# Attention without GpSimd: weights' lower halves on VectorE, probabilities scaled by ScalarE and VectorE

## The chip, the cores and the metric

The kernel runs on one core of a Trainium2 chip. The metric is the device time of one execution in microseconds. The kernel before has a median of 2958.11 us over three runs (2956.08 to 6801.14 us).

## The reference, cut to what matters

One inference step of a decoder trunk of four layers, for a prompt of 512 positions and a sample group of 8 rows: sparse attention (NSA), gMLP, HGRN2, sparse attention again, each followed by a SwiGLU FFN and layer norms. The change touches the two attention layers, and of these the prompt group. There are 16 query heads in 4 key-value groups of 4, of width 64. Each branch (compressed, selected, window) makes a masked softmax and adds its product with the values, times a gate:

```
s = einsum('bqgrd,bkgd->bqgrk', q, k) * ATTN_SCALE
p = where(mask, softmax(where(mask, s, NEG_INF)), 0)
o_branch = einsum('bqgrk,bkgd->bqgrd', p, v)
o = gates[0] * o_cmp + gates[1] * o_slc + gates[2] * o_win
```

With 512 positions every block of 64 is selected, so the selected and the window branch are plain causal attention over their own keys and values. The factor gate / sum of the softmax is applied to the probabilities.

## The kernel before, in words

Activations lie transposed: 128 features on the partitions, 520 columns (512 prompt positions and 8 sample rows) in two halves of 256 and 264. A matrix product in full precision is made of three TensorE passes over halves of the operands: upper by upper (L344), lower by upper (L345), upper by lower (L346). The upper half is a copy rounded to TensorE's format, the lower half what the rounding left out.

**Weights.** `Weights.need` (called by `mm` before each group of products) keeps a few parts of 512 columns split ahead of use (three in the attention layers, `ahead`). A part comes by DMA on SyncE's queue, `split` has ScalarE copy the upper half (L148) and at once, as `lag` is off there, another engine subtract (L150). That engine is VectorE, unless `self.sub` names another. In `nsa`, once tile 9 of the 21 tiles of the input projection is reached (L1507), `sub` names GpSimd for both parts of a tile, and it is set back after the output projection (L1532): the parts of u_in from tile 9 on, two for each tile, and the 16 of u_out.

**The order of work.** Each engine carries out its instructions in the order in which the program wrote them. The input projection (`mm`, 21 tiles, two halves) calls `tick` after every second k-step; a tick advances generators: `compress` (summaries of the cached pages, L1050 among them), from tile 9 on `attend`, four steps for each tick. So projection products, attention and splits lie between each other by the order of writing, not by readiness. When the projection is done, `attend` goes on beside `sample` (the 8 sample rows) and, with its later half, beside the output projection.

**Attention.** `attend` goes over 4 groups g, 4 query blocks qb of 128 and 3 branches. For the selected and the window branch `scores` handles four heads i: two score products (L1176) of n = 128, 256, 384 or 512 key columns, on VectorE the mask and the row minimum in one instruction (L1178; signs are turned), one step later on ScalarE the exp with its sum (L1180). Then VectorE makes reciprocal and factor (L1184, L1185), and each head's probabilities are multiplied by their factor: head 0 on GpSimd, head 1 on ScalarE (L1189), heads 2 and 3 on VectorE (L1192). This happens 32 times in a layer, eight times for each n. Two rounds later `mix` transposes the probabilities on TensorE (L1211), ScalarE takes the upper half out (L1214), VectorE the lower half (L1215), and TensorE multiplies by the values (L1227).

**Around it on VectorE:** the evacuation of keys (L1452 to L1457; L1453 and L1454 each subtract 64 x 256, L1454 reading the one operand from the upper and the other from the lower partitions), of queries (L1472, L1476), the compressed branch (L1149 to L1162), the split of the attention's result (L306) and residual sums (L488, L469). L1283 scales the probabilities of the sample rows.

Of the kernel before, what the change touches and what calls it, by code (L numbers as in the profile page):

```python
# [11 lines left out]
OP = mybir.AluOpType  # L12
# [51 lines left out]
def wait(n):  # L64
    for _ in range(n):
        yield
# [169 lines left out]
class Net:  # L236
# [773 lines left out]
    def nsa(self, layer, plan):  # L1010
        nc, a = self.nc, self.a
# [99 lines left out]
        def attend():  # L1111
# [3 lines left out]
            def defer(f):  # L1115
                due.append([DEFER, f])
# [49 lines left out]
            def scores(g, qb, br):  # L1166
                q0, n = qb * 128, qb * 128 + 128
                nn = max(n, 256)
                kt = K[g, br]
                Ps = [self.slot(), self.slot()]  # L1170
                st = self.small("nst", 8, bufs=4)
                for i in range(4):
                    p = self.ps()
                    q = Q[g, i // 2][:, i % 2, q0:n]
                    for s in range(2):
                        nc.tensor.matmul(p[:, :nn], q, kt[:, s, :nn], start=s == 0, stop=s == 1)  # L1176
                    P = Ps[i // 2][:, i % 2, :n]
                    nc.vector.tensor_tensor_reduce(P, p[:, :n], tri[:, 512 - n:], 1.0, 3e38, OP.add, OP.min,  # L1178
                                                   st[:, i:i + 1])
                    defer(lambda P=P, i=i: (self.table(LN_EXP), nc.scalar.activation(  # L1180
                        P, P, AF.Exp, bias=st[:, i:i + 1], scale=-1.0, accum_out=st[:, 4 + i:5 + i])))
                    yield
                yield from wait(DEFER)
                nc.vector.reciprocal(st[:, 4:8], st[:, 4:8])  # L1184
                nc.vector.tensor_mul(st[:, 4:8], st[:, 4:8], gt[:, qb, 16 * br + 4 * g:16 * br + 4 * g + 4])  # L1185
                for i in range(4):
                    P = Ps[i // 2][:, i % 2, :n]
                    if i == 1:
                        nc.scalar.activation(P, P, AF.Copy, scale=st[:, 4 + i:5 + i])  # L1189
                    else:  # L1190
                        eng = nc.gpsimd if i == 0 else nc.vector
                        eng.tensor_scalar(P, P, st[:, 4 + i:5 + i], None, op0=OP.mult)  # L1192
                D[g, qb, br] = Ps
                yield

# [47 lines left out]
            for g, qb, br in [(g, qb, br) for g in range(4) for qb in range(4) for br in range(3)]:  # L1243
                if qb == br == 0:
                    while g not in done or "prompt" not in done:
                        yield
                    oT[g] = self.slot()
                    late.append(values(g))
                late.append(mix(g, qb, br))
                cur = [scores(g, qb, br) if br else scores_cmp(g, qb)]  # L1250
                while len(late) > LAG:
                    cur.append(late.pop(0))
                for _ in alternate(cur[0], chain(*cur[1:])):
                    flush()
                    yield
# [230 lines left out]
        for i, (m, h) in enumerate(self.order(21, 6, 0)):  # L1486
            if i == 4:
                cst = self.small("ncst", 672)
                nc.scalar.dma_start(cst, a["nsa_cst"])
                tri = cst[:, :512]  # L1490
                cmask = cst[:, 512:640].rearrange("p (q c) -> p q c", q=4)
                valid = cst[:, 640:641]
                m8, gm = cst[:, 641:649], cst[:, 649:653]
                brsel, hsel = cst[:48, 653:656], cst[:48, 656:672]
                kcS = self.sm.tile([128, 2, 2, 9, 32], FT, name="kcS", tag="kcS", bufs=1)
                nc.gpsimd.memset(kcS, 0.0)
                zero = self.flat()
                nc.gpsimd.memset(zero, 0.0)
                KV, PTC2 = self.flat(FR), [self.slot(FR), self.slot(FR)]
                nc.vector.tensor_copy(KV, zero)  # L1500
                for t in PTC2:
                    nc.vector.tensor_copy(t.rearrange("p a b -> p (a b)"), zero)
                VC = KV[:, 512:1024].rearrange("p (g c) -> p g c", g=4)
                Qd = self.sm.tile([128, 2, 8, 16], FT, name="Qd", tag="Qd", bufs=1)
                nc.gpsimd.memset(Qd, 0.0)
            if m == 9 and h == 0:
                self.W.sub = (nc.gpsimd, nc.gpsimd)  # L1507
                att = self.spawn(attend(), RATE)
            p = self.mm(u_in[m], 8, X, h)
            evac(m, h, p)  # L1510
# [141 lines left out]
```

## Time and profile before

| | before |
|---|---|
| median of the runs | 2958.11 us |
| profiled execution | 2956.41 us |
| its span, first to last instruction | 2954.7 us |
| mean granted TensorE clock | 0.978 of full speed |
| instructions on TensorE, VectorE, ScalarE, GpSimd | 21806, 4377, 3586, 674 |

The profile is that of one execution. PE is TensorE's matmuls and PEld its weight loads, DVE VectorE, ACT ScalarE, POOL GpSimd, SP SyncE. L150 is line 150 of the kernel. Time points count from the span's start. Busy TensorE is not TensorE at its peak, since matmuls overlap. The first attention layer lies at about 15 to 440 us, the second at about 2120 to 2540 us. Two instructions on one engine can overlap by a little, so a pair can be shorter than twice one.

### The profile page before, as it was taken

What the parts mean: (1) busy time and instruction counts of PE and PEld (TensorE: products, weight loads), DVE (VectorE), ACT (ScalarE), POOL (GpSimd) and SP (SyncE); (2) the same over time, 40 slices, a digit from 0 to 9 for tenths busy, and PEclk for the clock granted to TensorE, in tenths of its full rate; (3) what the DMA queues carried; (4) which work ended last, traced back from release to release, by engine and by line L of the source; (5) the groups of instructions that cost most, each with busy time, mean ns of one, the idle gap of its engine ahead of it and who ended that gap; (6) DMA issues with size and microseconds to landing.
All of it is one profiled execution on the core that took longest, in us unless ns stands there. A gap on an engine that the chain in (4) does not pass through costs nothing.

```text
span 2954.7 us, 56446 instructions
## 1 busy us (share of the span) xinstructions
PE 2766.9 (94%) x21806; PEld 2642.0 (89%) x21806; DVE 2011.7 (68%) x4377; ACT 1591.5 (54%) x3586; POOL 731.9 (25%) x674
## 2 busy tenths in 40 slices
PE   7999888999999999999999989999899998899997
PEld 7888568999999899999999989999888875899997
DVE  5788757665766775677676677557768876575665
ACT  4666545554565464465455556446566655463553
POOL 0222141342321223232000022323112212322342
PEclk9999999999999999999999999999999999999998
DMA  5122533555523255562222235556122243445561
GB/s 180 65 65 70 181 121 94 144 154 147 154 79 102 61 138 138 139 185 80 81 88 81 71 93 143 140 139 190 60 83 65 65 160 123 118 114 137 148 158 53
DMA packets 167678, 340.38 MB, mean 115 GB/s; under 512 B 15474, under 2 KB 78450, under 8 KB 167410
## 3 DMA queue, kind: packets, MB, share of 16 engines
q1 hardware_dynamic: 147840, 281.79, 30.1%
q0 software_dynamic: 12096, 44.05, 8.6%
q10 hardware_dynamic: 7474, 10.95, 1.0%
q8 instruction: 171, 2.80, 0.4%
q14 instruction: 97, 0.79, 0.1%
HBM read 323.46 MB, written 13.27 MB: 114 GB/s over the span
## 4 chain that ended last, share of the span: by engine, by line
PE 71%; DVE 15%; ACT 9%; issue 2%; DMA 2%; SPq 1%; POOL 0%; ACTq 0%; POOLq 0%; DVEq 0%
PE ps L344 11%; PE ps L346 11%; PE ps L345 11%; PE ps L566 9%; PE ps L567 9%; PE ps L568 8%; PE ps L1050 2%; PE ps L1227 2%; PE ps L1176 1%; ACT g L1180 1%; DVE g L1178 1%; ACT g L380 1%; PE ps L873 1%; PE ps L1211 1%; DVE g L150 1%
## 5 line engine op out<-in xcount | busy, mean ns | idle before, releaser
L344 PE MATMUL ps<-g 128*128 128x256 f32 (+1 forms) x3744 | 1093.7, 292 | 26.8 <-ACT g L148 21.0
L346 PE MATMUL ps<-g 128*128 128x256 f32 (+1 forms) x3744 | 1071.3, 286 | 16.2 <-DVE g L411 14.3
L345 PE MATMUL ps<-g 128*128 128x256 f32 (+1 forms) x3744 | 1067.6, 285 | 5.6 <-DVE g L150 2.9
L344 PEld LDWEIGHTS ps<-g 128*128 128x128 f32 x3744 | 718.1, 192 | 41.8 <-ACT g L148 22.3
L346 PEld LDWEIGHTS ps<-g 128*128 128x128 f32 x3744 | 715.6, 191 | 19.7 <-DVE g L411 17.0
L345 PEld LDWEIGHTS ps<-g 128*128 128x128 f32 x3744 | 717.2, 192 | 12.7 <-DVE g L150 4.4
L150 DVE TENSOR_TENSOR g<-g 128x512 fp32r<-128x512 f32 x708 | 578.7, 835 | 152.1 <-ACT g L148 149.1
L566 PE MATMUL ps<-g 128*128 128x260 f32 x2128 | 601.8, 283 | 7.5 <-ACT frow L613 7.5
L567 PE MATMUL ps<-g 128*128 128x260 f32 x2128 | 601.6, 283 | 0.0
L568 PE MATMUL ps<-g 128*128 128x260 f32 x2128 | 601.1, 282 | 0.0
L148 ACT CAST g<-g 128x512 fp32r<-128x512 f32 (+1 forms) x788 | 460.6, 607 | 121.8 <-PE ps L346 86.9
L566 PEld LDWEIGHTS ps<-g 128*128 128x128 f32 x2128 | 401.2, 189 | 8.3 <-ACT frow L613 8.3
L568 PEld LDWEIGHTS ps<-g 128*128 128x128 f32 x2128 | 401.6, 189 | 0.0
L567 PEld LDWEIGHTS ps<-g 128*128 128x128 f32 x2128 | 401.1, 189 | 0.0
L613 ACT ACTIVATE frow<-ps 128x260 f32<-128x260 f32 x304 | 118.1, 388 | 245.8 <-PE ps L568 245.6
L1180 ACT ACTIVATE g<-g,nst 128x128 f32<-128x128 f32 (+3 forms) x256 | 143.1, 559 | 127.7 <-DVE nst L1178 125.5
L150 DVE TENSOR_TENSOR g<-fsum,g 128x512 fp32r<-128x512 f32 x228 | 163.4, 717 | 35.2 <-ACT g L148 35.2
L622 POOL TENSOR_TENSOR frow<-frow 128x260 f32<-128x260 f32 x64 | 47.9, 749 | 520.4 <-ACT frow L613 520.4
L150 POOL TENSOR_TENSOR g<-g 128x512 fp32r<-128x512 f32 x80 | 105.7, 1328 | 255.7 <-ACT g L148 249.4
L1192 POOL TENSOR_SCALAR g<-g,nst 128x128 f32<-128x128 f32 (+3 forms) x64 | 76.3, 1192 | 351.0 <-DVE nst L1185 243.4
L148 ACT CAST g<-fsum 128x512 fp32r<-128x512 f32 x228 | 133.9, 616 | 48.8 <-PE ps L346 48.8
L488 DVE SCALAR_TENSOR_TENSOR x<-x,ps 128x256 f32<-128x256 f32 (+1 forms) x128 | 53.2, 422 | 152.7 <-PE ps L346 152.7
(270 smaller groups left out, 4061.6 us busy)
## 6 DMA issues: line engine op xcount, KB each, us to landing
g<-ffn_in SPq DMA_DIRECT2D x176, 512.0 KB, 4.7
g<-ffn_in POOLq DMA_DIRECT2D x76, 512.0 KB, 5.9
g<-ffn_out SPq DMA_DIRECT2D x64, 448.0 KB, 3.8
g<-nsa_in SPq DMA_DIRECT2D x42, 512.0 KB, 4.0
fsum<-ffn_in SPq DMA_DIRECT2D x76, 256.0 KB, 3.5
cm<-cache_cmp SPq DMA_DIRECT2D x64, 256.0 KB, 3.7
g<-cache_slc SPq DMA_DIRECT2D x128, 128.0 KB, 2.5
g<-cache_win SPq DMA_DIRECT2D x32, 512.0 KB, 5.7
```

The lines of the kernel that those rows point to most:

```text
L148: self.nc.scalar.copy(h, src)
L150: self.subs.append(lambda: (eng or self.nc.vector).tensor_sub(l, src, h.bitcast(FT)))
L344: nc.tensor.matmul(p[:, :n], H[:, s], a, start=k == 0, stop=False)
L345: nc.tensor.matmul(p[:, :n], L[:, s], a, start=False, stop=False)
L346: nc.tensor.matmul(p[:, :n], H[:, s], b, start=False, stop=k == nk - 1)
L566: nc.tensor.matmul(p, H[:, s], a, start=start and k == 0, stop=False, skip_group_check=True)
L567: nc.tensor.matmul(p, L[:, s], a, start=False, stop=False, skip_group_check=True)
L568: nc.tensor.matmul(p, H[:, s], b, start=False, stop=k == 3, skip_group_check=True)
L613: nc.scalar.activation(s[q], p, AF.Copy, scale=-1.0 if q in (1, 5) else 1.0)
L1050: nc.tensor.matmul(p[:, :8 * n], WC[kv][:, l], cv[:, :n, kv, l, :], start=l == 0, stop=l == 7)
L1180: defer(lambda P=P, i=i: (self.table(LN_EXP), nc.scalar.activation(P, P, AF.Exp, bias=st[:, i:i + 1], scale=-1.0, accum_out=st[:, 4 + i:5 ...
L1192: eng.tensor_scalar(P, P, st[:, 4 + i:5 + i], None, op0=OP.mult)
```

## The change

Two places. In `scores`, head 0 is scaled by ScalarE, as head 1 is, and no longer by GpSimd; heads 2 and 3 stay on VectorE. In `nsa`, `sub` is no longer set, so that all lower halves of weights are subtracted by VectorE. Order of writing, tiles and DMAs stay as they are.

```diff
@@ -1185,11 +1185,10 @@
                 for i in range(4):
                     P = Ps[i // 2][:, i % 2, :n]
-                    if i == 1:
+                    if i < 2:
                         nc.scalar.activation(P, P, AF.Copy, scale=st[:, 4 + i:5 + i])
                     else:
-                        eng = nc.gpsimd if i == 0 else nc.vector
-                        eng.tensor_scalar(P, P, st[:, 4 + i:5 + i], None, op0=OP.mult)
+                        nc.vector.tensor_scalar(P, P, st[:, 4 + i:5 + i], None, op0=OP.mult)
@@ -1504,7 +1503,6 @@
             if m == 9 and h == 0:
-                self.W.sub = (nc.gpsimd, nc.gpsimd)
                 att = self.spawn(attend(), RATE)
```

## Rows read from the trace of the kernel before

**Rows 1.** the page: totals; groups (count, busy us, mean ns, idle before)
```profile
PE 2766.9 (94%) x21806; PEld 2642.0 (89%) x21806; DVE 2011.7 (68%) x4377; ACT 1591.5 (54%) x3586; POOL 731.9 (25%) x674
...
L150 POOL TENSOR_TENSOR g<-g 128x512 fp32r<-128x512 f32 x80 | 105.7, 1328 | 255.7 <-ACT g L148 249.4
L1192 POOL TENSOR_SCALAR g<-g,nst 128x128 f32<-128x128 f32 (+3 forms) x64 | 76.3, 1192 | 351.0 <-DVE nst L1185 243.4
```

**Rows 2.** windows: stretch, length, busy us (instructions) by engine, clock, DMA
```profile
85.00:300.00 215.00, 194.19 (x1383) 176.48 (x1383) 179.57 (x545) 142.02 (x373) 55.90 (x46) 0.98 0.22 66
300.00:400.00 100.00, 85.94 (x564) 59.88 (x563) 69.11 (x218) 55.76 (x144) 22.47 (x20) 0.93 0.49 151
```

**Rows 3.** the chain of waits, 85 to 300 us, by line
```profile
by line: ACT g L1180 8.6%; DVE g L1178 8.4%; PE ps L345 4.8%; PE ps L346 4.8%; issue 4.8%; PE ps L344 4.8%; PE ps L1227 4.7%; PE ps L1176 4.5%; DVE g L1454 4.5%; DVE g L1215 4.2%; PE ps L1050 4.2%; PE ps L1211 4.1%; DVE g L1192 3.9%; DVE g 
```

**Rows 4.** waits, 85 to 300 us: who <- for whom: us, times, longest
```profile
DVE nst L1184 <- ACT g L1180: 17.9, 24, 1.1
...
DVE g L1178 <- PE ps L1176: 1.9, 2, 1.0
...
ACT g L1180 <- DVE nst L1178: 42.3, 45, 3.7
...
PE ps L1211 <- POOL g L1192: 4.0, 2, 2.5
```

**Rows 5.** timeline, 202 to 205 us: start, us, engine, line, operation
```profile
202.67 0.62 ACT L148 CAST g<-g 128x512 fp32r<-128x512 f32 x1
...
202.62 0.28 DVE L1149 TENSOR_TENSOR g<-ps,ncst 128x128 f32<-128x128 f32 x1
...
203.47 1.28 DVE L1215 TENSOR_TENSOR g<-ps,g 128x512 fp32r<-128x512 f32 x2
```

**Rows 6.** timeline, 169 to 172 us, VectorE and GpSimd
```profile
169.79 1.40 DVE L1454 TENSOR_TENSOR g<-g 64x256 fp32r<-64x256 f32 x1
...
169.48 1.43 POOL L150 TENSOR_TENSOR g<-g 128x512 fp32r<-128x512 f32 x1 [2.68 <-PE ps L1176]
```

**Rows 7.** line groups with shapes kept apart, 60 to 440 us
```profile
L1454 DVE TENSOR_TENSOR g<-g 64x256 fp32r<-64x256 f32 x13 | 11.4, 877 | 0.2
...
L1453 DVE TENSOR_TENSOR g<-g 64x256 fp32r<-64x256 f32 x13 | 5.4, 418 | 0.4
...
L1283 DVE TENSOR_SCALAR g<-g,sst 128x513 f32<-128x513 f32 x2 | 1.0, 488 | 0.1
```

**Rows 8.** line groups with shapes together, 60 to 440 us
```profile
L1180 ACT ACTIVATE g<-g,nst 128x128 f32<-128x128 f32 (+3 forms) x128 | 71.5, 559 | 64.6 <-DVE nst L1178 63.6 <-DVE g L1380 0.7
...
L1192 DVE TENSOR_SCALAR g<-g,nst 128x128 f32<-128x128 f32 (+3 forms) x64 | 32.0, 542 | 1.1
...
L1189 ACT ACTIVATE g<-g,nst 128x128 f32<-128x128 f32 (+3 forms) x32 | 18.0, 563 | 14.8 <-DVE nst L1185 14.8
```

**Rows 9.** timeline: pairs of L1192 on VectorE, and GpSimd beside them
```profile
134.09 1.32 DVE L1192 TENSOR_SCALAR g<-g,nst 128x512 f32<-128x512 f32 x2
...
134.22 1.79 POOL L1192 TENSOR_SCALAR g<-g,nst 128x512 f32<-128x512 f32 x1 [1.11 <-DVE nst L1185]
...
162.83 0.48 DVE L1192 TENSOR_SCALAR g<-g,nst 128x128 f32<-128x128 f32 x2
...
166.04 0.60 DVE L1192 TENSOR_SCALAR g<-g,nst 128x128 f32<-128x128 f32 x2
...
254.84 1.63 DVE L1192 TENSOR_SCALAR g<-g,nst 128x256 f32<-128x256 f32 x2
...
254.99 1.33 POOL L150 TENSOR_TENSOR g<-g 128x512 fp32r<-128x512 f32 x1 [6.22 <-ACT g L148]
```

**Rows 10.** the chain of waits, 140 to 153 us, by line
```profile
by line: PE ps L1050 27.5%; PE ps L1227 14.4%; PE ps L346 13.9%; PE ps L1211 13.4%; PE ps L344 13.0%; PE ps L345 13.0%; PE ps L1144 6.7%
```

**Rows 11.** waits, 400 to 440 us, and VectorE's timeline there
```profile
PE ps L345 <- POOL g L150: 1.3, 1, 1.3
...
427.21 4.02 DVE L306 TENSOR_TENSOR g<-g 128x528 fp32r<-128x528 f32 x4
```

## The prediction

> **What bounds the kernel now.** I read the totals first. TensorE is busy for 94% of the span, VectorE for 68%, ScalarE for 54% and GpSimd for 25% [rows 1]. The same page prices what moves: over both attention layers GpSimd spends 105.7 us on 80 lower halves of weights (1.33 us each) and 76.3 us on 64 scalings (1.19 us each). That GpSimd has time to spare says nothing of whether it is in the way, so the second view is the first attention layer itself, cut into stretches [rows 2]: 85 to 300 us, where projections and attention run together, and 300 to 400 us, where attention, the sample group and the start of the output projection share the engines; up to 440 us the projection ends. In the first, VectorE works 179.6 of 215 us, its highest share, and TensorE 194.2. So I asked who is late. The chain of waits there carries exps (ScalarE, 8.6%), row minima (VectorE, 8.4%), VectorE's L1454, L1215 and L1192, and projection matmuls in turn [rows 3]: three engines pass the end between them. The waits give the direction [rows 4]: VectorE waits 17.9 us for exps and only 1.9 us for scores from TensorE, while ScalarE waits 42.3 us in 45 places for VectorE. VectorE and ScalarE are the tight pair in this stretch; TensorE is slack where they are on the chain and sets the end where it isn't. The second layer repeats the first; I work out one and double it.
>
> **Moving the lower halves (L150).** Per layer 40 leave GpSimd: 24 for u_in tiles 9 to 20, which with the run-ahead fall mostly into the first stretch, and 16 for u_out. No DMA moves. VectorE does one in 0.68 us, or 0.60 from start to start (L1215, the same shape) [rows 5]. The price is not that time alone. L150 stands directly behind ScalarE's cast L148 in the program, and VectorE takes its queue in order, so VectorE must wait for the cast while minima, reciprocals and lower halves of probabilities are queued behind it. In [rows 5] the cast ends at 203.29 and VectorE's next instruction, L1149, began at 202.62: it would begin at 203.29 + 0.60 = 203.89, 1.27 us later. I take 1.27 us for each place that counts.
>
> Which count? Six of the 24 stand beside an L1454. There the trace shows GpSimd's own cost: L1454 takes 1.40 us while L150 runs on GpSimd [rows 6], against 0.418 us for its sister L1453; 11.4 us for 13 with 0.42 as the undisturbed value makes (11.4 - 13 x 0.42) / 1.0 = 6 stretched ones [rows 7]. Two more stand beside a stretched 256-column pair of L1192, 1.63 us [rows 9] instead of the 0.84 that lies between the pairs of 128 and 512 columns. At these eight, 1.27 us come and about 1.0 us goes: nothing. Twelve stand in stretches such as 140 to 153 us, where the chain is TensorE alone [rows 10]; the cover is TensorE's run of L1050 and projections, and if it is gone each costs 1.27 us. That leaves four: **+5.1 us**. Of the rest, six fall into the second stretch, where VectorE is busy 69% only [rows 2]; I count one, **+1.3 us**. In the third stretch the move helps: TensorE waits 1.3 us for GpSimd, and four L306 take 4.02 us instead of some 4 x 0.60 [rows 11]. With two of the moved instructions standing near them I take **-2.0 us**. The ends: 0 (all hidden) and 16 x 1.27 = 20.3 us in the first stretch.
>
> **Scaling without GpSimd (L1189, L1192).** Head 0 goes from GpSimd to ScalarE; heads 2 and 3 stay on VectorE. VectorE loses no instruction, but it loses a neighbour. With GpSimd beside it a pair takes 0.60 us at 128 columns and 1.32 us at 512; another 128-column pair took 0.48 us [rows 9]. A VectorE scaling of 513 columns elsewhere takes 0.488 us [rows 7], so an undisturbed 512-column pair is at most 0.98 us. That is 0.12 to 0.34 us a pair, interpolated for the widths between: 0.92 us for one of each width, 7.4 us for the eight sets of a layer. On the chain L1192 has 3.9% of 215 us = 8.4 us [rows 3], against three quarters of its 32.0 us [rows 8], since three of the four groups of heads lie in this stretch: a share of 0.35, so **-2.6 us**; ends 0 and -7.4.
>
> The Trainium skill (SBUF — State Buffer, section on SBUF's two separate sides) says that VectorE, in a mode with two ports or with two SBUF inputs, and GpSimd take a shared port pair in turn, the loser blocked for the whole instruction. By that rule the relief would be complete wherever they meet. The trace agrees for L1454 (1.40 us, ending 0.28 us after GpSimd's 1.43 us) and not for L1192: its 512-column pair ends after 1.32 us though the scaling that GpSimd began beside it takes 1.79 us [rows 9], so nothing blocked it to the end.
>
> ScalarE gains 32 scalings of 0.563 us, 18.0 us a layer [rows 8]. Behind each stand casts (L1214, L1202, L148) and the next exps. In 45 places ScalarE then waits 0.94 us on average for VectorE [rows 4], of the 96 exps that three groups of heads make, so about half swallow the 0.56 us. Of the other half I count ScalarE's share on the chain: exps hold 8.6% of 215 = 18.5 us of their 54 us (three quarters of 71.5) [rows 3, 8], 0.34. So 18.0 x 0.5 x 0.34 = **+3.1 us**, ends 0 and 18.0.
>
> The same skill (ScalarE: Activation LUTs, rules for kernel authors) sends multiplications to VectorE and so speaks against this half of the change. By it head 0 would cost VectorE at most 0.49 us and ScalarE nothing, and the 3.1 us would turn into a price on the tighter engine, of at most 32 x 0.49 x 0.35 = 5.5 us a layer; I keep the term as it is.
>
> Last, TensorE's transposes wait 4.0 us for GpSimd's scaling, 2.5 us of it at once [rows 4]. GpSimd's scaling ends 1.19 us after the factors are ready, but 1.33 us later where an L150 got in ahead of it, as at 254.99 [rows 1, 9]; two ScalarE scalings end after 2 x 0.563 = 1.13 us. I take **-3.0 us**.
>
> **Sum per layer:** 5.1 + 1.3 - 2.0 - 2.6 + 3.1 - 3.0 = +1.9 us; both, +3.8 us. The profiled execution took 2956.41 us (span 2954.7), which makes 2960.2 us; the median shown, 2958.11, is 1.7 us above it, so I say **2962 us**: large moves that nearly cancel.
>
> **The rivals.** *GpSimd was the brake* (faster). If relief counts in full wherever the engines meet: -7.4 for L1192, -4.0 for the transposes, -2.5 at the end of the layer, and of the L150 only one in the open, +1.3: -12.6 us a layer, **2933 us**. The rule on the shared port (above) is what would make it so. For it: L1454 and L1192 together hold 8.4% of the chain [rows 3]. Against it: six of the stretched instructions get an L150 put before them. *VectorE becomes the pacer* (slower). If VectorE's order decides in TensorE's stretches too, which it does once what VectorE is behind by outlasts TensorE's run of 12 us [rows 10], 16 places pay: 20.3 - 7.4 + 9 (half of ScalarE's addition, for whose casts the L150 then wait) - 4.0 - 1.0 = +16.9 us a layer, **2992 us**. For it: 179.6 of 215 us busy and no wait for TensorE to speak of [rows 2, 4]. Against: those stretches show TensorE alone. That the change does nothing is no rival: engines are named in the code.
>
> **How the numbers follow.** Forecast 0.53, GpSimd the brake 0.24, VectorE the pacer 0.23. The range goes 5 us past both rivals' centres, which leaves out somewhat under half of each: 2928 to 2998 us. A verdict needs 2%, 59 us (below 2899 or above 3017), about what a measurement of this kernel can tell from no change. Only the extreme ends reach that: 20.3 + 18.0 without relief is +77 us over both layers; complete relief, 6 us at L1454 with it and nothing given back, is some -40. So faster 0.02, same 0.94, slower 0.04.
>
> **What would show it.** After: no L150 and no L1192 on GpSimd; L1454 at 0.42 us in all places; the 512-column pair of L1192 under 0.98 us, and if it stays at 1.32 the relief term is wrong; VectorE's waits for L148 of 0.6 to 1.3 us before L150 in the first stretch; ScalarE up by about 36 us, VectorE up by 80 x 0.68 = 54 us less some 27 us of relief; no wait of L1211 for GpSimd. The stretch from 85 us, up to the same matmul, should be within 5 us of 215. The prediction is wrong if the pushes behind L148 show up as TensorE's waits for minima (L1178) well over the present ones, or if the layer shrinks by over 8 us.

## The result, and the profile after

The kernel after takes 2985.01 us (median of four runs, 2983.2 to 2986.27) against 2957.1 us. The ratio is 1.0102 [1.0086, 1.0117], so the change makes the kernel 1.0% slower, about 30 us, which is less than 2%. One run of 6801.14 us of the kernel before is left out of the ratio; its three others have a mean of 2954.6 us. The profiled execution took 2983.2 us (span 2980.3), with a mean granted clock of 0.974.

The totals on the page of the kernel after (busy us, share of the span, instructions):

```profile
PE 2781.7 (93%) x21806; PEld 2654.8 (89%) x21806; DVE 2023.6 (68%) x4457; ACT 1618.6 (54%) x3650; POOL 555.1 (19%) x530
```

Against [rows 1], VectorE does 80 instructions more and is busy only 11.9 us longer. 80 x 0.69 = 55 us came, so some 43 us went: most of it lies in two groups of old instructions, shown below, that take less time now that GpSimd has nothing to do beside them. By busy time alone the change costs VectorE next to nothing.

Now the stretch of [rows 2], to the same matmul. At 316.29 us stands the L1050 group that began at 296.61 us in before, and at 319.7 us the stretch has done what before had done at 300.1. Windows of the kernel after (start:end, length, busy us by PE, PEld, DVE, ACT, POOL, clock, DMA share, GB/s); the second window ends at the place that was 440.1 us in before:

```profile
87.00:319.70 232.70, 204.02 (x1383) 182.99 (x1382) 176.57 (x561) 152.44 (x399) 0.75 (x1) 0.94 0.20 61
319.70:451.80 132.10, 116.44 (x814) 84.33 (x814) 92.16 (x269) 69.86 (x171) 8.53 (x8) 0.97 0.51 163
```

The same two windows of the kernel before:

```profile
85.00:300.10 215.10, 194.29 (x1384) 176.58 (x1384) 179.59 (x545) 142.09 (x374) 56.00 (x46) 0.98 0.22 66
300.10:440.10 140.00, 120.65 (x815) 86.86 (x814) 84.07 (x247) 66.29 (x162) 39.13 (x35) 0.94 0.48 153
```

The first stretch grew by 17.6 us, though VectorE works 3.0 us less in it, with 20 L150 more. The second gave 7.9 us back. (In the second layer the first stretch went from 214.1 to 229.8 us.) By the same matmuls, the two stretches of both layers hold 18.4 of the 25.6 us between the two profiled executions. Another 2.0 us lie ahead of 85 us, where the first moved subtractions stand, and 5.1 us between the two attention layers, in work that the change does not touch. The profile of a faster version below (e3) is longer by as much there, so these 5 us cannot be put down to the change.

What VectorE does with the longer time stands in the waits of the kernel after, 87.0 to 319.7 us (who <- for whom: us, times, longest):

```profile
ACT g L1180 <- DVE nst L1178: 39.7, 37, 3.5
DVE g L150 <- ACT g L148: 20.0, 14, 2.0
DVE nst L1184 <- ACT g L1180: 15.8, 22, 1.0
...
DVE g L1178 <- PE ps L1176: 3.5, 3, 1.6
...
DVE g L1451 <- ACT g L1448: 3.1, 6, 0.9
DVE g L1471 <- ACT g L1467: 3.0, 3, 1.4
```

The first row of VectorE was not there before: L150 waits for the cast L148, 1.43 us on average. All of VectorE's waits for ScalarE in this stretch together are 28.0 us in before and 44.8 us in after. (From L1192 on, lines are one lower than in before.)

One such place, VectorE and then ScalarE (start, us, engine, line, operation; in brackets idle before, and for whom). It is the place of [rows 5], shifted: L1149 is what stands behind the L150.

```profile
211.85 0.75 DVE L1191 TENSOR_SCALAR g<-g,nst 128x384 f32<-128x384 f32 x2
214.05 0.69 DVE L150 TENSOR_TENSOR g<-g 128x512 fp32r<-128x512 f32 x1 [1.46 <-ACT g L148]
214.66 0.28 DVE L1149 TENSOR_TENSOR g<-ps,ncst 128x128 f32<-128x128 f32 x1
...
211.91 1.12 ACT L1189 ACTIVATE g<-g,nst 128x384 f32<-128x384 f32 x2 [0.50 <-DVE nst L1185]
212.94 0.57 ACT L1213 CAST g<-ps 128x512 fp32r<-128x512 f32 x1
213.40 0.62 ACT L148 CAST g<-g 128x512 fp32r<-128x512 f32 x1
```

VectorE is done with its two scalings at 212.60. ScalarE, which now also has two, begins them no earlier than VectorE does, then makes a cast for `mix`, then the weight's cast, and VectorE stands still until that is done: 1.46 us. Both halves of the change meet here.

The chain of waits of the kernel after, where [rows 10] showed TensorE alone (the same part of the work, 147 to 160 us), and then in the whole stretch of [rows 3]:

```profile
by line: DMA cm<-cache_cmp 24.9%; issue 14.7%; DVE g L150 11.0%; ACT g L1189 10.3%; DVE g L1471 10.1%; SPq L1007 6.9%; SPq L1008 6.5%; ACT g L1467 5.8%; ACT g L1180 5.5%; ACT g L148 4.8%; DVE kcS L1058 4.2%; SPq L134 2.6%; DVE Qd L1475 2.5%
...
by line: ACT g L1180 10.9%; DVE g L1178 8.3%; ACT g L1189 6.6%; issue 5.9%; DVE g L150 4.8%; DVE g L1214 4.5%; PE ps L1226 3.5%; ACT g L148 3.3%; PE ps L1050 3.1%; DMA cm<-cache_cmp 2.8%; PE ps L1176 2.7%; PE ps L1210 2.6%; PE ps L344 2.0%;
```

TensorE's run is not on the first chain any more, and the projection's L344 holds 2.0% of the second instead of 4.8%. That another engine is on the chain does not yet say that time was lost there; the section on the prediction comes back to this place.

VectorE's groups in the first layer of the kernel after, 60 to 460 us (busy us, mean ns | idle before, releaser):

```profile
L150 DVE TENSOR_TENSOR g<-g 128x512 fp32r<-128x512 f32 x44 | 31.4, 716 | 31.2 <-ACT g L148 31.0
L1191 DVE TENSOR_SCALAR g<-g,nst 128x128 f32<-128x128 f32 (+3 forms) x64 | 22.4, 393 | 1.1
L1453 DVE TENSOR_TENSOR g<-g 64x256 fp32r<-64x256 f32 x14 | 5.9, 419 | 0.2
```

The scalings fell from 32.0 to 22.4 us [rows 8], and L1453 (L1454 of before) from 0.877 to 0.419 us each [rows 7]. Before L150 VectorE is idle for as long as L150 works.

### The profile page after: what moved, and what is told of

Read it like the earlier page. It is cut to its first block, busy times and chain, and to the rows that moved or that the text cites. A ratio compares the mean times of both kernels' runs of the same rounds, so it can differ in the third digit from the quotient of the medians.

```text
span 2980.3 us, 56243 instructions
## 1 busy us (share of the span) xinstructions
PE 2781.7 (93%) x21806; PEld 2654.8 (89%) x21806; DVE 2023.6 (68%) x4457; ACT 1618.6 (54%) x3650; POOL 555.1 (19%) x530
## 4 chain that ended last, share of the span: by engine, by line
PE 67%; DVE 16%; ACT 12%; issue 3%; DMA 2%; SPq 0%; ACTq 0%; POOLq 0%; POOL 0%; DVEq 0%
PE ps L344 10%; PE ps L346 10%; PE ps L345 10%; PE ps L566 8%; PE ps L567 8%; PE ps L568 8%; DVE g L150 2%; ACT g L1180 2%; ACT g L148 2%; DVE g L1178 1%; PE ps L873 1%; ACT g L380 1%; PE ps L1050 1%; ACT g L1189 1%; DVE x L402 1%
## 5 line engine op out<-in xcount | busy, mean ns | idle before, releaser
L344 PE MATMUL ps<-g 128*128 128x256 f32 (+1 forms) x3744 | 1097.3, 293 | 29.9 <-ACT g L148 20.9
L346 PE MATMUL ps<-g 128*128 128x256 f32 (+1 forms) x3744 | 1073.3, 287 | 14.5 <-DVE g L411 13.2
L150 DVE TENSOR_TENSOR g<-g 128x512 fp32r<-128x512 f32 (+1 forms) x788 | 635.2, 822 | 211.9 <-ACT g L148 208.4
L344 PEld LDWEIGHTS ps<-g 128*128 128x128 f32 x3744 | 720.8, 193 | 46.1 <-ACT g L148 22.1
L148 ACT CAST g<-g 128x512 fp32r<-128x512 f32 (+1 forms) x788 | 460.6, 607 | 122.5 <-PE ps L346 87.5
L150 DVE TENSOR_TENSOR g<-fsum,g 128x512 fp32r<-128x512 f32 x228 | 163.5, 717 | 35.3 <-ACT g L148 35.3
L148 ACT CAST g<-fsum 128x512 fp32r<-128x512 f32 x228 | 133.9, 616 | 48.6 <-PE ps L346 48.6
L1226 PE MATMUL ps<-g 128*128 128x512 f32 x384 | 145.8, 458 | 7.5 <-DVE g L1214 7.4
L183 POOL TENSOR_TENSOR fsum<-g 128x512 f32<-128x512 f32 x76 | 120.7, 1589 | 123.7 <-DMA g<-ffn_in 123.7
```

Of the source, the lines that this page charges most:

```text
L148: self.nc.scalar.copy(h, src)
L150: self.subs.append(lambda: (eng or self.nc.vector).tensor_sub(l, src, h.bitcast(FT)))
L183: nc.gpsimd.tensor_add(t[x], t[p], t[q])
L344: nc.tensor.matmul(p[:, :n], H[:, s], a, start=k == 0, stop=False)
L346: nc.tensor.matmul(p[:, :n], H[:, s], b, start=False, stop=k == nk - 1)
L1226: nc.tensor.matmul(o, v, PT[:, s, :512], start=start and s == 0, stop=stop and s == 1)
```

## The experiments

Three theories, called theory 1 to 3 in the expectations. **The order (T1):** the time lies in VectorE standing still before each L150 until ScalarE has made the cast written just ahead of it. **The load (T2):** it lies in VectorE's additional work. **ScalarE (T3):** it lies in ScalarE's second scaling, which delays casts and exps. All ratios are to the kernel before on the same chip; medians of different experiments can come from different chips, so differences are worked out from the ratios.

**Each half alone.** Only the lower halves to VectorE (`scores` as before):

```diff
-                self.W.sub = (nc.gpsimd, nc.gpsimd)
```

> The kernel before with one half of the change: lower halves of weights by VectorE, head 0 still scaled by GpSimd. Theory 1 (order: VectorE stands still for ScalarE's cast L148 before each L150, and the pairs minima-exps run late): most of the 28 us is here, 2978 to 2990 us, and VectorE's waits for L148 in the first stretch near the 21 us of the changed kernel. Theory 2 (load: VectorE has 27 us more work a layer): the same time, so this run doesn't tell 1 from 2. Theory 3 (ScalarE's second scaling delays casts and exps): nearly nothing, 2955 to 2962 us. L1192's pairs should stay slow (1.32 us at 512 columns), as GpSimd still scales beside them.

Only head 0 to ScalarE (`sub` as before):

```diff
-                    if i == 1:
+                    if i < 2:
```

> The kernel before with the other half: head 0 scaled by ScalarE, lower halves of weights still by GpSimd. Theories 1 and 2: no slower than before, 2945 to 2958 us, since VectorE's scaling pairs shrink (0.5 us each at 512 columns) and TensorE's 4 us a layer of waits for GpSimd's scaling go. Theory 3: the bulk of the loss, 2972 to 2985 us.

The first gave 1.0049 [1.0032, 1.0065], the second 1.0019 [1.0008, 1.003]: 14.5 and 5.6 us, together 20 of the 30. About 10 us come only when both are done; by the three intervals this can be anything from some 3 to 17 us. No theory forecast both times: the first is below the 2978 to 2990 us of T1 and T2, and the second is above the 2958 us of T1 and T2 and below the 2972 us of T3. In the first alone L150 waits 228.9 us for L148 over the whole kernel, in after 243.7, in before 184.3 (255, 255 and 211 places):

```profile
DVE g L150 <- ACT g L148: 228.9, 255, 10.8
```

With head 0 alone on ScalarE VectorE has none of these L150, and it waits longer for other casts instead. Its two evacuations (L1451 and L1471 here) wait 16.3 us for them, against 9.2 us in before (waits, 86.1 to 306.2 us):

```profile
DVE nst L1184 <- ACT g L1180: 16.8, 23, 1.0
DVE g L1451 <- ACT g L1448: 8.4, 12, 1.1
DVE g L1471 <- ACT g L1467: 7.9, 8, 1.3
```

**The order put right.** The kernel after, with the subtraction of each part written only when the next part's cast is written (`lag`, which the kernel has for another layer), from tile 9 to the end of `nsa`. All work stays where the change put it.

```diff
+                self.W.lag = True
                 att = self.spawn(attend(), RATE)
...
+        self.W.flush()
+        self.W.lag = False
```

> The changed kernel, but in the attention each L150 is written one part later, behind the next part's cast, so that its own cast is long done when VectorE comes to it; work is the same. Theory 1 (VectorE standing still for L148): the 21 us of waits in the first stretch vanish and the layer gets 8 to 14 us back, 2957 to 2970 us. Theory 2 (load): the waits vanish and the time hardly moves, 2978 to 2986 us. Theory 3: no change, 2985 us.

0.9961 [0.9949, 0.9974], 2943.1 us: the whole loss is gone and a little more, also more than the 2957 to 2970 us that T1 forecast. Windows and timeline of this kernel, the same stretch and the same place as above:

```profile
85.60:298.50 212.90, 195.20 (x1384) 173.66 (x1383) 176.67 (x564) 152.06 (x397) 0.73 (x1) 0.99 0.22 67
...
200.32 0.75 DVE L1191 TENSOR_SCALAR g<-g,nst 128x384 f32<-128x384 f32 x2
200.98 0.68 DVE L150 TENSOR_TENSOR g<-g 128x512 fp32r<-128x512 f32 x1
201.58 0.28 DVE L1149 TENSOR_TENSOR g<-ps,ncst 128x128 f32<-128x128 f32 x1
...
201.87 0.62 ACT L148 CAST g<-g 128x512 fp32r<-128x512 f32 x1
```

VectorE's busy time is that of after (176.67 and 176.57), ScalarE's too (152.06 and 152.44), and the stretch is 19.8 us shorter. L150 follows the scalings at once, and the cast that lies beside it, at 201.87, is the next part's. T1 holds; T2 and T3, as causes by themselves, are excluded by this run, since their work is all still there. Over the kernel the waits for L148 fell from 243.7 to 185.3 us, and the time by 0.0141 x 2955 = 41.7 us: 0.71 us for each us of waiting taken away.

The Trainium skill (PSUM — Partial Sum Buffer, section on engine and sequencer instructions) says that the queues of ScalarE, VectorE and GpSimd are strictly first in, first out. The two timelines agree: L1149, which needs nothing of the weight, begins 2.06 us after the scalings' end in after, and 0.51 us after it here.

**The control.** The same two lines of `lag` on the kernel before.

> The kernel before, with each L150 on GpSimd written one part later. Nobody stands behind GpSimd's wait except its own scalings, so theory 1 expects little: 2948 to 2960 us. If writing the lower halves later helps whichever engine makes them, it gains like the lagged changed kernel, 40 us against nothing: below 2935 us.

1.0026 [1.0014, 1.0038], 2960.87 us. `lag` is no gain in itself, as T1 had it within a microsecond: where GpSimd makes the subtractions, VectorE does not wait for these casts (its waits for L148 over the kernel are nearly those of e3), and there is nothing to take away.

**Where head 0 belongs.** In the kernel after, head 0 to VectorE instead of ScalarE:

```diff
-                    if i < 2:
+                    if i == 1:
```

> The changed kernel with head 0 scaled by VectorE too: three scalings on VectorE, one on ScalarE, nothing on GpSimd. ScalarE loses 18 us a layer, VectorE gains 32 times some 0.3 us, 9 to 10 us a layer. Theory 3 (ScalarE): faster, 2965 to 2978 us. Theory 2 (VectorE's load): slower, 2990 to 3005 us. Theory 1: casts L148 come 0.5 us sooner but VectorE is 0.3 us later at each set; within 6 us of the changed kernel.

1.0058 [1.0042, 1.0074], 2970.42 us: 0.0044 x 2955 = 13 us better than after, though VectorE works more. That lies in T3's range and outside T1's 6 us. Windows and waits of this kernel:

```profile
87.00:316.00 229.00, 200.55 (x1384) 180.34 (x1383) 183.36 (x586) 142.66 (x375) 0.74 (x1) 0.96 0.20 62
...
DVE g L150 <- ACT g L148: 13.9, 15, 1.3
```

6.8 us more work on VectorE and 6.1 us less waiting for L148, 10.3 us less for ScalarE in all. T3 is true as far as this: ScalarE's second scaling costs by lengthening the wait that T1 names. The same with `lag` (this line in e3):

> The lagged kernel (each L150 one part later) with head 0 scaled by VectorE as well, one head on ScalarE. In the unlagged kernel this swap was worth 15 us. If it was worth that because ScalarE's second scaling made the casts L148 late for a waiting VectorE (theory 1, with ScalarE feeding the wait), it is now worth little or costs: 2940 to 2952 us. If ScalarE's queue is late by itself (theory 3), the gain stays: 2925 to 2935 us.

0.9972 [0.9963, 0.9981], beside 0.9961 for e3: no better. The stretch takes 212.90 us in both, 182.8 busy + 20.8 waiting here, 176.7 + 27.9 there. This is T1's forecast. And with head 0 on GpSimd as before, the lower halves on VectorE with `lag` (e1 with the two lines of e3):

> Lagged lower halves on VectorE, head 0 scaled by GpSimd as before the change. Against the lagged kernel it puts back GpSimd's slowing of VectorE's scaling pairs (7 us of VectorE's time a layer) and TensorE's waits for GpSimd's scaling, and takes ScalarE's second scaling away. If the contention weighs more: 2950 to 2962 us; if ScalarE's scaling weighs more: 2930 to 2940 us.

0.9968 [0.9958, 0.9977], 2945.41 us, between the two ranges that were forecast; the stretch takes 212.5 us. With the order right it makes no measurable difference which engine scales head 0.

The Trainium skill (ScalarE: Activation LUTs, rules for kernel authors) would have multiplications on VectorE and not on ScalarE. Without `lag` the runs agree, by 13 us; with `lag` they show no such gain.

**The load by itself.** e3 with every subtraction of these weights done twice on VectorE (the result stays the same):

```diff
-        self.subs.append(lambda: (eng or self.nc.vector).tensor_sub(l, src, h.bitcast(FT)))
+        self.subs += [lambda: (eng or self.nc.vector).tensor_sub(l, src, h.bitcast(FT))] * (2 if self.twice else 1)
```

> The lagged kernel with each L150 of the attention done twice on VectorE (the same numbers once more): 40 times 0.60 us, 24 us a layer of load and no further wait. Theory 1 (the wait counts, load is mostly hidden): 2950 to 2965 us. Theory 2 (load counts one for one): 2985 to 2995 us. It gives the price of VectorE's time by itself.

1.0075 [1.006, 1.0089], 2973.98 us. Totals and stretch:

```profile
PE 2774.6 (93%) x21806; PEld 2644.4 (89%) x21806; DVE 2077.4 (70%) x4537; ACT 1618.3 (54%) x3650; POOL 554.7 (19%) x530
...
85.40:312.00 226.60, 200.96 (x1383) 178.65 (x1382) 190.94 (x586) 152.22 (x399) 0.72 (x1) 0.96 0.20 63
```

VectorE is busy 56.1 us longer than in e3 (2021.3), and the time is 0.0114 x 2955 = 33.7 us longer: 0.60 us for each us of work, and between the ranges of T1 and T2. In the stretch 14.3 us of work made 13.7 us of length. So VectorE's work does set this stretch's length, and T2 has the right price. It failed on the amount: the change's own work was paid for by the relief.

**All kernels in one account.** In the first stretch the length comes out, in each kernel, as VectorE's busy time, its waits for ScalarE and for TensorE, and 5 to 8 us of gaps between instructions (sums over all rows of VectorE in the waits view, one profiled execution each):

| | length | busy | waits for ScalarE | for TensorE | rest |
|---|---|---|---|---|---|
| before | 215.1 | 179.6 | 28.0 | 2.2 | 5.3 |
| e2, scaling only | 220.1 | 174.3 | 36.7 | 2.6 | 6.5 |
| e1, weights only | 228.8 | 182.8 | 34.5 | 5.3 | 6.2 |
| after | 232.7 | 176.6 | 44.8 | 3.5 | 7.8 |
| e4, head 0 on VectorE | 229.0 | 183.4 | 34.5 | 5.1 | 6.0 |
| e3, after with lag | 212.9 | 176.7 | 27.9 | 1.9 | 6.4 |
| e5, e4 with lag | 212.9 | 182.8 | 20.8 | 3.1 | 6.2 |
| e6, e1 with lag | 212.5 | 182.1 | 21.0 | 3.1 | 6.3 |
| e7, before with lag | 215.6 | 179.0 | 27.9 | 2.3 | 6.5 |
| e8, e3 twice | 226.6 | 190.9 | 24.9 | 4.0 | 6.8 |

That busy, waits and gaps add up is so for any engine. What the table shows is that VectorE's waits are for ScalarE and hardly for TensorE. That the sum sets the length is shown by the edits: e3 takes waits away and the stretch shrinks by about as much, e8 adds work and it grows by about as much. That makes VectorE with ScalarE the pacer here, though TensorE is busy for 194 us of before's 215. Two limits: ScalarE itself waits 9.6 us in before for TensorE's transposes (L1214 for L1211), so some of VectorE's waits for ScalarE may be TensorE's at second hand; and e1's profile is of the slowest of its six runs (2975.95 us, median 2969.09), so its row is rather too long.

**A version that beats both.** e3 with `lag` on from the start in all layers, not in attention alone:

```diff
-        self.lag, self.subs = False, []
+        self.lag, self.subs = True, []
```

(and the other settings of `lag` removed).

> The lagged kernel with the lag on in all layers, not in attention and the paired products alone. Outside the attention VectorE still waits 184 us for L148, the same in all kernels so far. If a wait costs wherever VectorE stands still: 2850 to 2910 us. If it costs only where VectorE and ScalarE are the tight pair, as the attention's first stretch, and TensorE covers it elsewhere: 2938 to 2950 us, though VectorE's waits for L148 fall by far.

0.9872 [0.9856, 0.9889], 2915.07 us. That is 0.0089 of before's time below e3, 26 us, and between the two ranges that were forecast. VectorE's waits for L148 fell by another 78 us to 107.2, and TensorE paid some of it back, waiting now for lower halves that come late (waits over the whole kernel):

```profile
DVE g L150 <- ACT g L148: 107.2, 153, 12.4
...
PE ps L345 <- DVE g L150: 31.7, 15, 4.9
```

The two traces show where it lies. From the matmul that ends the first attention layer's output projection to the one where the second layer's first stretch begins, e3 takes 1751.2 us (436.8 to 2188.0) and this kernel 1724.4 us (435.7 to 2160.1): 26.8 of the 29.8 us by which its profiled execution is shorter. The two attention layers hold 1.2 us of it.

## Why the prediction was right or wrong

The time fell into the range (2928 to 2998 us) and the change is within 2%, as forecast. That is luck of a wide range, which reached past both rivals: the sum behind the 2962 us is wrong. 2985 us lies 23 us above it and 7 us below the 2992 us of the rival *VectorE becomes the pacer*. That rival names the right pacer, but it puts the loss into TensorE's runs, and the traces show most of it elsewhere.

**The step that failed** is the price of a place: "I take 1.27 us for each place that counts." The prediction counted 24 places in the stretch; it holds 20 L150 in after. Eight of them stand in the two long runs of TensorE (147 to 162 and 231 to 246 us). The other twelve, as many as the prediction had outside the runs (four that pay, eight that pay nothing), all wait for their cast: 16.2 of the 20.0 us, 1.35 us each. With the 0.69 us of the subtraction a place costs VectorE 2.04 us, not 1.27. Twelve such places are 24.5 us where the prediction's price makes 15.2, and the eight were not cancelled by "about 1.0 us" each. The 1.27 us came from one place in [rows 5], where the cast ended 0.67 us after VectorE was ready. Over all 14 waits the mean is 1.43 us, up to 2.0, where the prediction named 0.6 to 1.3 us. In e1 and e4, where ScalarE makes one scaling and not two, it is 0.93 us (13.9 us in 15 places). So ScalarE's second scaling, which stands ahead of the cast, made the wait longer. The prediction priced that scaling by exps and casts on the chain, +3.1 us a layer, and not by the wait of its own other half.

**The cover** held better than the chain of the kernel after suggests. TensorE in the place of [rows 10], in before and then in after:

```profile
141.31 1.95 PE L1050 MATMUL ps<-cm,g 128*128 128x128 f32 x16
147.05 1.03 PE L1144 MATMUL ps<-g 128*128 128x192 f32 x8
...
147.49 1.95 PE L1050 MATMUL ps<-cm,g 128*128 128x128 f32 x16
153.22 1.56 PE L1144 MATMUL ps<-g 128*128 128x192 f32 x8
162.78 0.50 PE L1226 MATMUL ps<-g 128*128 128x512 f32 x1 [1.37 <-DVE g L1214]
```

From the first L1050 to L1144 TensorE takes 5.7 us in both, though VectorE stands still for 1.96 us beside it. Only at the run's end does TensorE wait, 1.37 us for VectorE's L1214. The L1050 at 141.31 us in before comes 6.2 us later in after, and the L1144 at 164.07 us comes 8.2 us later: TensorE lost 2.0 us in this run and at its end. By the same account it lost 1.5 us in the other run (218.99 and 241.93 us in before), and the other 14.1 us in the rest of the stretch. So eight covered places cost 3.5 us together, where the prediction had nothing and "1.27 us each" would make 10.2. The chain itself is a poor witness. In e3, whose stretch is 2.2 us shorter than that of before, TensorE is not on the chain of this part either; in e8, 13.7 us longer than e3, it is (chains of e3, 140 to 153 us, and of e8, 142 to 155 us):

```profile
by line: DVE g L1471 12.3%; ACT g L1180 11.8%; ACT g L1467 11.7%; ACT g L1189 10.3%; DVE g L1214 9.2%; ACT g L148 8.8%; DVE kcS L1058 8.5%; DVE g L1235 5.7%; DVE g L150 5.3%; issue 5.2%; DVE g L1149 2.3%; DVE g L1151 2.3%; DVE g L1157 2.3%;
...
by line: PE ps L1050 27.5%; PE ps L346 10.2%; PE ps L345 9.3%; PE ps L344 9.3%; DVE g L1214 9.2%; PE ps L1210 6.8%; PE ps L1144 6.7%; DVE g L1471 6.5%; DVE kcS L1058 4.2%; PE ps L1226 3.6%; DVE g L1149 2.3%; DVE g L1151 2.3%; DVE g L1152 2.
```

The hint at the pacer stood in [rows 2, 4], and the rival quoted it: VectorE is busy for 179.6 of 215 us and next to never waits for TensorE. Some 10 us of the whole loss come only with both halves of the change. The longer wait of L150 fits them, 243.7 us over the kernel against 228.9 in e1. The first stretch of the first layer does not show them by itself (13.7 and 5.0 us for the halves, 17.6 for both); that of the second layer does (8.6 and 2.7 us, and 15.7 for both). With e1's profile the slow one named above, how much of the 10 us stands in these stretches stays open.

**The relief was too low as well, and that is why the loss wasn't worse.** "0.92 us for one of each width, 7.4 us" a layer at most: L1192 alone gave 32.0 - 22.4 = 9.6, and -2.6 had been counted. L1454 gave the expected fall to 0.42 us in all places (6.0 us for the 12 of the stretch), which the sum had taken to cancel with L150s. VectorE rose by 11.9 us where 27 had been named. In the first stretch the relief bought the work: 20 L150 brought 13.8 us, and L1192 (24.5 to 16.7 us) and L1454 (11.0 to 5.0) took 13.8 away; the other 3.0 us were not taken apart. The wait remained: +17.6 us = -3.0 (busy) + 16.8 (waits for ScalarE) + 1.3 (for TensorE) + 2.5 (rest).

**The end of the layer.** Second stretch and end together were put at 1.3 - 2.0 = -0.7 us, and gave -7.9. Four L306 as in [rows 11] went from 4.02 to 2.57 us:

```profile
440.85 2.57 DVE L306 TENSOR_TENSOR g<-g 128x528 fp32r<-128x528 f32 x4
```

The rest is not settled. VectorE's waits for scores in this window fell from 17.8 to 7.6 us, but in e3, with the same relief, they are 16.0 us, and the window takes 138.3 us. Only after and e4 are short there (132.1 and 132.9 us). A late end of the first stretch does not explain it alone, since e1 and e8 end late too and take 137.3 and 138.1 us; nor does GpSimd's absence, which e3 and e8 share.

**Marks.** Right: no L150 and no L1192 on GpSimd, L1454 at 0.42 us, and no wait of L1211 for GpSimd (in its place 3.0 us for L1189 and 3.5 for L1451, so the -3.0 us had a new wait behind it). The 512-column pair, forecast "under 0.98 us", took 0.88:

```profile
141.04 0.88 DVE L1191 TENSOR_SCALAR g<-g,nst 128x512 f32<-128x512 f32 x2
```

Wrong: the stretch within 5 us of 215; ScalarE up by 36 us (27.1, since two scalings in a row overlap: 64 took 32.5 us a layer, where 32 took 18.0). And the mark named for failure did not show: TensorE's waits for minima (L1178) in the stretch are 11.9 us in before and 9.8 in after. TensorE's loss appears as 9.7 us more busy time for the same matmuls, at a granted clock of 0.94 instead of 0.98, and as 7.9 us more of short waits.

## What to carry to other kernels

When one engine's output is taken by a second whose queue runs in order, the price of moving the second half is the wait at its place in that queue and not its busy time alone; here 43 us of relief paid for most of 55 us of work, and 59 us of waiting decided. Write the taking instruction one part later than the giving one: the same work on the same engines went from 1.0102 to 0.9961. And add up, for the stretch in question, each engine's busy time and whom its waits are for: an engine that hardly ever waits for the one that is "94% busy" is a candidate for the pacer, and an edit that adds work to it (e8) or takes waits from it (e3) tells. Which engine a chain shows in a short window is no measure of what a place costs: compare when the same matmul starts in both kernels.

## What the runs showed of the hardware that was not expected

VectorE's scaling pairs of 512 columns, all in place on one tile each, took 1.32 us beside GpSimd's scaling [rows 9] and 0.88 us without it, a factor of 1.5. Over both layers the neighbour cost VectorE some 43 us, more than half of the 80 x 0.69 us of work that GpSimd took off it with the weights.

The two half changes part the neighbours. In e1 GpSimd still scales but makes no lower half: the scalings stay slow and L1454 is fast. In e2 GpSimd makes lower halves but does not scale: L1453 (L1454 of before) stays slow. Groups of the first layer, 60 to 455 us, in e1 (two lines), e2 and after:

```profile
L1192 DVE TENSOR_SCALAR g<-g,nst 128x512 f32<-128x512 f32 x16 | 10.6, 702 | 0.3
L1454 DVE TENSOR_TENSOR g<-g 64x256 fp32r<-64x256 f32 x14 | 5.9, 419 | 0.2
...
L1453 DVE TENSOR_TENSOR g<-g 64x256 fp32r<-64x256 f32 x14 | 11.8, 844 | 0.2
...
L1191 DVE TENSOR_SCALAR g<-g,nst 128x512 f32<-128x512 f32 x16 | 7.7, 521 | 0.3
```

The Trainium skill (SBUF — State Buffer, section on SBUF's two separate sides) describes the contention of VectorE and GpSimd as a lock that blocks the loser for the whole instruction. For L1454, 1.40 us then and 0.42 us now, the runs agree. For the scalings they show a slowing and no full block: from after to e1 the mean of one rises from 284 to 314 ns at 128 columns and from 521 to 702 ns at 512, by 11% and 35%. There the measurement decides.
